# Mixer groups as steps placed by column tile, in a one-core decoder layer

## The chip, the cores and the metric

The kernel runs on one core of a Trainium2 chip. The metric is device time in microseconds (us) of one execution; of several runs the median is given. A core has five engines that run side by side and wait for one another through semaphores: PE (matrix products), DVE (elementwise), ACT (elementwise with functions), POOL (elementwise), and SP, which here issues the DMA transfers. Each engine takes its instructions strictly in the order of its own queue.

## What is computed

One decoding step of one hybrid layer, for 256 prompt tokens and 8 sampled sequences of one token, 264 columns in all: a half feed-forward step, a mixer, a second half feed-forward step, and a gated per-layer embedding. The mixer is what matters here:

```python
proj = u @ w_in
glu_a, glu_b, z, xbc, dt_raw = jnp.split(proj, [s1, s2, s3, s4], axis=-1)
v = glu_a * jax.nn.sigmoid(glu_b)
v, new_conv_buf = causal_dwconv(v, conv_buf, conv_mod_w, conv_mod_b)     # 31 taps
v = jax.nn.silu(layernorm(v, conv_mod_ln_g, conv_mod_ln_b))
xbc, new_xbc_buf = causal_dwconv(xbc, xbc_buf, ssm_conv_w, ssm_conv_b)   # 4 taps
xbc = jax.nn.silu(xbc)
xs, bm, cm = jnp.split(xbc, ...)
y, h_new = ssd(xs, dt, a, bm, cm, d_skip, h0r)
yg = y * jax.nn.silu(z)
yg = yg * lax.rsqrt(jnp.mean(yg * yg, axis=-1, keepdims=True) + EPS)     # in 8 groups
out = jnp.concatenate([v, yg * ssm_norm_g], axis=-1) @ w_out
```

`ssd` is a chunked state-space scan in 8 groups of 6 heads. For the sampled sequences it multiplies the incoming state of 64x128 per head (`h0`) with C and sums over the 128 state columns.

## The kernel before

**Matrix products.** Activations lie with channels on the 128 partitions and the 264 columns along the free axis. The weights come from memory in the order in which a list, PLAN, uses them, one unit of 16 tiles of 128x128 at a time, in two pieces of 8 tiles: SP loads a piece into `wraw`, ACT casts it into `whi` (line 152), and DVE takes the rest `wlo` = `wraw` - `whi` (line 153). Each of the three has four buffers, so the cast of a piece can begin once PE is through the piece four before it. A product of one weight tile is three matmuls (lines 248, 249, 250): `whi` with both parts of the activation and `wlo` with the first. A piece is thus 24 matmuls, and one column tile of the input projection (128 output channels over 2048 inputs) is 48. Its result is an `acc` in PSUM, of which there are five buffers.

**The input projection.** `IN_ORDER` lists its 81 column tiles: dt first, then for each of the 8 groups one tile B, one C, three x and three z. After the first x tile of the groups in `GLU_IN` stands a pair of tiles for the GLU (gb and ga), and the pairs left over come after the last group. What is done with each tile stands in the loop at lines 810 to 850. `do_conv` (line 610) reads an `acc` of B, C or x, does the 4-tap convolution on ACT and DVE and ends in a SiLU on ACT. `decays` (line 677) loads and makes the decay factors `ab` and `ea` of a group after its first x tile (DMA, ACT with Exp). After the third x tile `ssd` (line 698) does the whole group: transposes of x and B on PE (lines 708, 709), the product of B and C (722), chunk states (734), outputs (749, 756), then for the sampled sequences two transposes that give the rows of B and C (762, 763), a trip of these rows through memory to spread C over all partitions (766, 768), the product of state and C on POOL and its sum on DVE (774, 775), and the small rest. `gate` (line 790) multiplies `y` with SiLU(z) on DVE, squares three tiles on ACT (into `run` and two `tmp`), adds them on POOL into `run`, sums `run` over the channels on PE (`SumSq.total`, line 300, a matmul with a matrix of ones), takes the root through Ln and Exp on ACT and applies it. It is called for a group after the first x tile of the next one.

**GLU.** `do_glu` (line 641) takes Exp, Ln and Exp of one pair, multiplies, and puts 30 further taps of the 31-tap convolution on a list `bg`. Four entries of that list are done after each column tile, ten after each output column of the output projection. Behind the last pair's taps stands `do_ln`, the LayerNorm over the eight GLU tiles. Their first reader is the last part of the output projection (line 882).

**What sets the order.** The program text gives each instruction its priority. A scheduler that keeps a timeline of its own lays the instructions into the five queues before the run: an engine takes, of what that timeline has ready, the instruction that stands first in the text, and the weights' loads, casts and subtractions go ahead of the rest. Functions of ACT that need a table (Silu, Sigmoid, Exp, Ln) are tied to the order of the text among themselves (`after`, line 223), and a table is loaded whenever the set changes (line 236). PSUM tiles of the pool `ps` (three buffers) are handed out in the order of the text.

## Time and profile before

| | us |
|---|---|
| median of 3 runs | 2439.51 (2439.47 to 2445.9) |
| the profiled execution | 2438.53 |
| its span, first to last instruction | 2436.7 |
| input projection of the mixer, about | 842 to 1345 |
| output projection, its main part, about | 1345 to 1494 |

The span is what the views of the profile show; the execution's own time has 1.8 us around it. In a row of the stages stand the length, then for PE, PE's weight loads, DVE, ACT and POOL the busy time and the number of instructions, then the clock that PE was granted, the share of the DMA engines and GB/s. A list of waits names the engine that waited with the line of its instruction, whom it waited for, the total, how often, and the longest.

### The profile page before, as it was taken

The page shows a single profiled execution, that of the slowest core. Times are in us where ns is not written, and L with a number is a line of the kernel's source. Part 1 is how long each engine was busy: PE and PEld are TensorE (multiplying, and loading weights), DVE is VectorE, ACT ScalarE, POOL GpSimd, SP SyncE. Part 2 cuts the span into 40 slices and gives each one's busy share as a digit, 9 for nine tenths or more (in the row PEclk, how much of TensorE's full clock was granted, in tenths as well). Part 3 has the DMA queues.
Part 4 walks back from the last instruction along what each step waited for, and adds up shares of the span by engine and source line. Part 5 has one row for each costly group of instructions (what it writes and reads, how often), then busy time and mean ns, then how long its engine had stood idle before and what let it go on. Part 6 is the DMA issues. An engine that isn't in the chain of part 4 may idle for free.

```text
span 2436.7 us, 47389 instructions
## 1 busy us (share of the span) xinstructions
PE 2370.0 (97%) x19444; PEld 2343.4 (96%) x19444; DVE 1577.0 (65%) x2273; ACT 1181.7 (48%) x1765; POOL 349.8 (14%) x351
## 2 busy tenths in 40 slices
PE   8999999999999999999999999899999999999988
PEld 8999999999999899999999999899999999999988
DVE  6554455545557858979798975866555565565595
ACT  6444444433456465565655555544444443344464
POOL 2500000000015212121121011400000000000142
PEclk9999999999999999999999999999999999999999
DMA  7656555555556666676666556477766676676653
GB/s 245 215 184 184 183 183 183 183 184 183 184 170 207 210 197 191 208 222 204 205 215 197 181 178 226 139 239 235 232 208 226 227 241 217 217 234 203 192 177 132
DMA packets 165386, 489.89 MB, mean 201 GB/s; under 512 B 25472, under 2 KB 42544, under 8 KB 165168
## 3 DMA queue, kind: packets, MB, share of 16 engines
q1 hardware_dynamic: 165168, 486.86, 62.1%
q8 instruction: 152, 2.49, 0.4%
q14 instruction: 66, 0.54, 0.1%
HBM read 465.65 MB, written 22.42 MB: 200 GB/s over the span
## 4 chain that ended last, share of the span: by engine, by line
PE 81%; DVE 7%; DMA 4%; issue 3%; ACT 2%; POOL 1%; SPq 0%; POOLq 0%; ACTq 0%; DVEq 0%
PE acc L248 26%; PE acc L249 26%; PE acc L250 26%; DVE wlo L153 3%; DVE y L217 1%; DMA d_bc<-rows 1%; DMA cbc<-d_bc 1%; POOL h L214 1%; DMA s<-in_hst 1%; DMA h<-in_hst 1%; DVE h L214 1%; DVE tmp L217 1%; ACT whi L152 1%; POOL run L214 1%; DVE act L217 1%
## 5 line engine op out<-in xcount | busy, mean ns | idle before, releaser
L250 PE MATMUL acc<-act,wlo 128*128 128x264 f32 x6320 | 1796.6, 285 | 4.4 <-DVE wlo L153 4.2
L249 PE MATMUL acc<-act,whi 128*128 128x264 f32 x6320 | 1783.7, 283 | 14.7 <-DVE act L217 7.8
L248 PE MATMUL acc<-act,whi 128*128 128x264 f32 x6320 | 1767.6, 283 | 16.6 <-ACT whi L152 8.7
L153 DVE TENSOR_TENSOR wlo<-wraw,whi 128x1024 fp32r<-128x1024 f32 (+1 forms) x806 | 994.9, 1236 | 584.9 <-ACT whi L152 580.7
L152 ACT CAST whi<-wraw 128x1024 fp32r<-128x1024 f32 (+1 forms) x806 | 829.0, 1033 | 945.2 <-PE acc L249 698.4
L248 PEld LDWEIGHTS acc<-act,whi 128*128 128x128 f32 x6320 | 1191.8, 190 | 19.9 <-ACT whi L152 8.9
L249 PEld LDWEIGHTS acc<-act,whi 128*128 128x128 f32 x6320 | 1188.6, 188 | 20.4 <-DVE act L217 10.0
L250 PEld LDWEIGHTS acc<-act,wlo 128*128 128x128 f32 x6320 | 1187.3, 188 | 8.1 <-DVE wlo L153 6.1
L214 POOL TENSOR_TENSOR run<-run,tmp 128x264 f32<-128x264 f32 x135 | 129.6, 960 | 956.0 <-ACT tmp L241 952.5
L214 POOL TENSOR_TENSOR s<-s,eap 128x1024 f32<-128x1024 f32 x24 | 46.4, 1932 | 598.8 <-DMA s<-in_hst 598.8
L217 DVE SCALAR_TENSOR_TENSOR y<-v,vec,y 128x251 f32<-128x251 f32 (+23 forms) x240 | 117.3, 512 | 1.2
L217 DVE SCALAR_TENSOR_TENSOR s<-bb,xds,s 128x128 f32<-128x128 f32 x192 | 52.6, 347 | 72.8 <-POOL s L214 72.8
L214 POOL TENSOR_TENSOR h<-h,cbc 128x512 f32<-128x512 f32 x48 | 72.2, 1524 | 167.4 <-DMA cbc<-d_bc 79.6
L256 ACT CAST act<-tmp 128x264 fp32r<-128x264 f32 x120 | 48.7, 411 | 72.8 <-DVE tmp L214 58.5
L214 DVE TENSOR_TENSOR tmp<-acc,rr 128x264 f32<-128x264 f32 x104 | 44.8, 431 | 56.8 <-PE acc L250 56.8
L214 DVE TENSOR_TENSOR tmp<-tmp,acc 128x264 f32<-128x264 f32 x88 | 37.7, 428 | 40.4 <-PE acc L250 39.4
L214 DVE TENSOR_TENSOR act<-tmp,act 128x264 fp32r<-128x264 f32 x120 | 54.3, 458 | 0.0
L241 ACT ACTIVATE tmp<-tmp 128x264 f32<-128x264 f32 x112 | 47.1, 422 | 10.2 <-DVE tmp L214 9.7
L241 ACT ACTIVATE tmp<-y 128x264 f32<-128x264 f32 x67 | 28.1, 426 | 43.6 <-DVE y L214 42.5
L214 DVE TENSOR_TENSOR y<-y,acc 128x264 f32<-128x264 f32 x80 | 34.0, 425 | 23.5 <-PE acc L250 23.5
L775 DVE TENSOR_REDUCE ych<-h 128x4 f32<-128x512 f32 x48 | 32.5, 678 | 20.0 <-POOL h L214 20.0
L217 DVE SCALAR_TENSOR_TENSOR act<-h,vec,act 128x264 fp32r<-128x264 f32 x48 | 35.2, 756 | 6.1 <-ACT act L241 6.1
(155 smaller groups left out, 787.2 us busy)
## 6 DMA issues: line engine op xcount, KB each, us to landing
wraw<-in_w SPq DMA_DIRECT2D x774, 512.0 KB, 4.7
h<-in_hst SPq DMA_DIRECT2D x48, 256.0 KB, 4.0
s<-in_hst SPq DMA_DIRECT2D x24, 512.0 KB, 6.8
out_nss<-s SPq DMA_DIRECT2D x24, 512.0 KB, 2.8
wraw<-in_w SPq DMA_DIRECT2D x32, 256.0 KB, 3.9
ab<-d_cs SPq DMA_DIRECT2D x16, 384.0 KB, 4.8
cbc<-d_bc SPq DMA_DIRECT2D x8, 512.0 KB, 4.3
bb<-d_bc SPq DMA_DIRECT2D x8, 512.0 KB, 8.3
```

The source lines that it names most:

```text
L152: nc.scalar.copy(hi, raw)
L153: nc.vector.tensor_tensor(out=lo, in0=raw, in1=hi.bitcast(F32), op=ALU.subtract)
L214: return (eng or nc.vector).tensor_tensor(out=out, in0=in0, in1=in1, op=op)
L217: return nc.vector.scalar_tensor_tensor(out=out, in0=in0, scalar=scalar, in1=in1, op0=op0, op1=op1)
L241: i = nc.scalar.activation(out=out, in_=in_, func=func, bias=bias, scale=scale)
L248: nc.tensor.matmul(acc, hi, x[:, 0, :], start=first, stop=False)
L249: nc.tensor.matmul(acc, hi, x[:, 1, :], start=False, stop=False)
L250: nc.tensor.matmul(acc, lo, x[:, 0, :], start=False, stop=last)
L256: nc.scalar.copy(t[:, 0, :], x)
L775: nc.vector.tensor_reduce(out=ych[:, j, b : b + 4], in_=h0, op=ALU.add, axis=AX.X)
```

## The change

The part of `ssd` for the sampled sequences becomes functions of its own (`sample_rows`, `sample_c`, `sample_state`, `sample_out`), `gate` becomes `gate_begin` and `gate_end`, and an object for each group, made at its B tile, places these steps at numbers of column tiles: a step that is placed at `n` stands in the text behind the tile `n`. The rows of B and C are made at the C tile and no longer behind the group's other work; C is spread two tiles later; the products of state and C take three tiles, each one's sum standing one tile behind its product; `ssd` comes one tile after the third x tile; and the gate comes after the group's own last z tile, in two tiles, and no longer behind the first x tile of the next group. GLU pairs stand in the groups 1, 3 and 5 only, so five pairs and no longer four follow the last group.

```diff
-GLU_IN = (1, 2, 4, 6)
+GLU_IN = (1, 3, 5)
...
-        if i < len(GLU_IN) + 2:
+        if yp is None:
             v = apool.tile([P, T], F32, tag="v", bufs=2, name=nm("v"))
...
         tt(y[:, :, P:NP_], y[:, :, P:NP_], ea, ALU.add)
-
-        js = slice(3 * g, 3 * g + 3)
+        return y
+
+    def sample_rows(g, bf, cf):
+
         pr = ps_tile([P, 2, P])
         nc.tensor.transpose(pr[:NS, 0, :], bf[:, NP_:], ident)
         nc.tensor.transpose(pr[:NS, 1, :], cf[:, NP_:], ident)
         rows = mp.tile([P, 2, P], F32, tag="rows", bufs=1, name=nm("rows"))
         nc.scalar.copy(rows[:NS], pr[:NS])
         nc.sync.dma_start(d_bc[g].rearrange("i b n -> b i n"), rows[:NS])
+
+    def sample_c(g):
         cbc = mp.tile([P, NS, P], F32, tag="cbc", bufs=1, name=nm("cbc"))
         nc.sync.dma_start(cbc, d_bc[g, 1].partition_broadcast(P))
-        ych = mp.tile([P, 3, NS], F32, tag="ych", bufs=1, name=nm("ych"))
-        for j in range(3):
-            for b in range(0, NS, 4):
-                h0 = mp.tile([P, 4, P], F32, tag="h0", bufs=3, name=nm("h0"))
-                nc.sync.dma_start(h0, a["hst"][3 * g + j][:, b : b + 4, :])
-                tt(h0, h0, cbc[:, b : b + 4, :], ALU.mult, nc.gpsimd)
-                nc.vector.tensor_reduce(out=ych[:, j, b : b + 4], in_=h0, op=ALU.add, axis=AX.X)
+        return cbc
+
+    products = []
+
+    def sample_state(g, j, cbc, ych):
+
+        while products:
+            o, h0 = products.pop(0)
+            nc.vector.tensor_reduce(out=o, in_=h0, op=ALU.add, axis=AX.X)
+        if j == 3:
+            return
+        for b in range(0, NS, 4):
+            h0 = mp.tile([P, 4, P], F32, tag="h0", bufs=3, name=nm("h0"))
+            nc.sync.dma_start(h0, a["hst"][3 * g + j][:, b : b + 4, :])
+            tt(h0, h0, cbc[:, b : b + 4, :], ALU.mult, nc.gpsimd)
+            products.append((ych[:, j, b : b + 4], h0))
+
+    def sample_out(g, bf, cf, xt, ych, y):
...
-        return y
-
-    def gate(g, y, zs):
+
+    def gate_begin(g, y, zs):
+
         tt(y, y, zs, ALU.mult)
         sq = SumSq(3, direct=0)
         for j in range(3):
             sq.add(y[:, j, :])
+        return sq
+
+    def gate_end(g, y, sq):
         t = tmp()
         rsqrt(t, sq.total(), eps1, 1.0 / 384)
...
+    class Group:
+
+
+        def __init__(self, g):
+            self.g = g
+            self.bc = mp.tile([P, 2, T], F32, tag="bc", bufs=2, name=nm("bc"))
+            self.xt = self.zs = None
+            place = {k: n for n, k in enumerate(IN_ORDER)}
+            c = place[("C", MT_CM + g)]
+            x, z = (place[(k, m + 3 * g + 2)] for k, m in (("x", MT_X), ("z", MT_Z)))
+            at(place[("x", MT_X + 3 * g)], self.decays)
+            at(c, lambda: sample_rows(g, *self.pair()))
+            at(c + 2, self.sample_c)
+            for j in range(4):
+                at(c + 3 + j, lambda j=j: self.state(j))
+            at(x + 1, self.ssd)
+            out = max(c + 6, x + 2)
+            at(out, self.out)
+            begin = max(out, z) + 1
+            at(begin, self.begin)
+            at(begin + 1, self.end)
...
-            if j == 0:
-                finish_gate()
-                ab, ea = decays(g)
-            if j == 2:
-                y = ssd(g, bct[:, 0, :], bct[:, 1, :], xt, ab, ea)
...
+        for step in steps.pop(n, ()):
+            step()
         for _ in range(4):
             if bg:
                 bg.popleft()()
```

What the scheduler makes of it is seen in the queues. First PE at the sum of the gate of the fifth group, before the change (`run` holds the squares added up, `whi_0_13867` is the piece in use, `ps_13756` and `ps_13765` take the transposes of the next group's x):

```order
L249 MATMUL acc_13928<-act_9304,whi_8_13692 128x264
L250 MATMUL acc_13928<-act_9304,wlo_8_13693 128x264
L248 MATMUL acc_13990<-act_9190,whi_0_13867 128x264
L249 MATMUL acc_13990<-act_9190,whi_0_13867 128x264
L300 MATMUL ps_13573<-run_13564,ones 128x264
L708 MATMUL ps_13756<-ident,h_13555 128x128
L708 MATMUL ps_13765<-ident,h_13555 128x128
L250 MATMUL acc_13990<-act_9190,wlo_0_13868 128x264
```

And ACT at the squares that this sum needs, before the change (the squares are the functions of `h_13038`):

```order
L152 CAST whi_0_13867<-wraw_0_13866 128x1024
L152 CAST whi_8_13873<-wraw_8_13872 128x1024
L241 ACTIVATE run_13564<-h_13038 128x264
L241 ACTIVATE tmp_13566<-h_13038 128x264
L241 ACTIVATE tmp_13569<-h_13038 128x264
L152 CAST whi_0_13930<-wraw_0_13929 128x1024
L152 CAST whi_8_13936<-wraw_8_13935 128x1024
L241 ACTIVATE tmp_13572<-ps_13573,eps_83 128x264
```

PE has the sum two matmuls into the piece `whi_0_13867`, while ACT has the squares only behind the next piece, `whi_8_13873`. The same two places of the change, PE first (the two transposes behind the sum are now those of the rows of B and C):

```order
L250 MATMUL acc_13533<-act_9214,wlo_0_13380 128x264
L248 MATMUL acc_13533<-act_9222,whi_0_13379 128x264
L300 MATMUL ps_13351<-run_13274,ones 128x264
L764 MATMUL ps_13371<-ident,bc_13265 8x128
L765 MATMUL ps_13371<-ident,bc_13265 8x128
L249 MATMUL acc_13533<-act_9222,whi_0_13379 128x264
```

Then ACT, after the change:

```order
L152 CAST whi_0_13379<-wraw_0_13378 128x1024
L241 ACTIVATE ab_13457<-ab_13457,acs 128x128 x6
L241 ACTIVATE bc_13265<-bc_13265 128x264
L236 ACT_TABLE_LOAD
L241 ACTIVATE run_13274<-h_12993 128x264
L241 ACTIVATE tmp_13276<-h_12993 128x264
L241 ACTIVATE tmp_13279<-h_12993 128x264
L152 CAST whi_8_13385<-wraw_8_13384 128x1024
L615 COPY xo_12565<-acc_13377 128x11
```

The squares have moved ahead by a piece against the sum: both stand in `whi_0_13379`, the sum thirteen matmuls into it.

The second place is the third x tile's transposes of the fourth group. PE before the change (`h_12006` holds the group's x, `whi_0_12443` is the piece in use):

```order
L248 MATMUL acc_12573<-act_9206,whi_0_12443 128x264
L249 MATMUL acc_12573<-act_9206,whi_0_12443 128x264
L250 MATMUL acc_12573<-act_9206,wlo_0_12444 128x264
L708 MATMUL ps_12207<-ident,h_12006 128x128
L708 MATMUL ps_12216<-ident,h_12006 128x128
L248 MATMUL acc_12573<-act_9214,whi_0_12443 128x264
L708 MATMUL ps_12207<-ident,h_12006 128x128
L709 MATMUL ps_12207<-ident,bc_11863 128x128
```

And after it (`h_11885` is the x, `whi_8_12233` the piece in use):

```order
L249 MATMUL acc_12437<-act_9270,whi_8_12233 128x264
L708 MATMUL ps_12291<-ident,h_11885 128x128
L709 MATMUL ps_12291<-ident,bc_11712 128x128
L708 MATMUL ps_12300<-ident,h_11885 128x128
L709 MATMUL ps_12300<-ident,bc_11712 128x128
L250 MATMUL acc_12437<-act_9270,wlo_8_12234 128x264
```

ACT at the SiLU of that tile, after the change (the last function of `h_11885`):

```order
L152 CAST whi_0_12227<-wraw_0_12226 128x1024
L241 ACTIVATE h_11885<-h_11885 128x264
L152 CAST whi_8_12233<-wraw_8_12232 128x1024
L152 CAST whi_0_12362<-wraw_0_12361 128x1024
L152 CAST whi_8_12368<-wraw_8_12367 128x1024
L241 ACTIVATE h_11885<-h_11885 128x264
```

Before the change the second and third tile's transposes stand within one another, in the piece just behind that of the first; after it the third stands alone, and its SiLU comes two casts behind the piece that PE uses at that place.

More of the change, by code (lines that the diff above doesn't have):

```diff
@@ L809, with at, last, group @@
+    steps = {}
+    def at(n, step):
+        steps.setdefault(n, []).append(step)
+    yctx = ctx.enter_context(ExitStack())
+    yp = None
+    def last():
+        nonlocal yp
+        mctx.close()
+        yp = yctx.enter_context(tc.tile_pool(name="yp", bufs=1))
+    first = gemm_first(us, k16, 4)
+    groups = {}
+    def group(g):
+        if g not in groups:
+            groups[g] = Group(g)
+        return groups[g]
     nglu = 0
@@ L840 @@
             nglu += 1
-            if nglu == len(GLU_IN) + 1:
-                finish_gate()
-                mctx.close()
-                yctx = ctx.enter_context(ExitStack())
-                yp = yctx.enter_context(tc.tile_pool(name="yp", bufs=1))
             if nglu == CM:
                 bg.append(do_ln)
+        for step in steps.pop(n, ()):
+            step()
         for _ in range(4):
@@ L850 @@
                 bg.popleft()()
+    assert not steps
     for k in range(CM + 16, CM + 24):
```

44 lines of the change are left out of this document (29 added, 15 removed).

## The prediction

> **What bounds the kernel now.** I read the page first, then the stage that the change touches, then who is waited for in it.
>
> ```profile
> span 2436.7 us, 47389 instructions
> PE 2370.0 (97%) x19444; PEld 2343.4 (96%) x19444; DVE 1577.0 (65%) x2273; ACT 1181.7 (48%) x1765; POOL 349.8 (14%) x351
> core 0: us, PE busy (x) PEld busy (x) DVE busy (x) ACT busy (x) POOL busy (x), PEclk, DMA share, GB/s
> 842.00:1345.00 503.00, 482.62 (x3918) 466.10 (x3916) 408.43 (x699) 291.93 (x530) 96.08 (x72) 0.99 0.66 204
> 1345.00:1494.00 149.00, 148.60 (x1232) 148.15 (x1232) 117.19 (x196) 78.54 (x117) 14.34 (x14) 1.00 0.58 184
> 1400.00:1420.00 20.00, 20.00 (x169) 20.00 (x168) 19.80 (x38) 8.04 (x9) 0.75 (x1) 1.00 0.55 185
> ```
>
> PE is the bound of the whole kernel. The change lies in the input projection of the mixer, about 842 to 1345 us; there PE is busy 482.6 of 503 us and DVE 408 (81%), so 20.4 us is all that idle PE time can give back, 0.8% of the kernel. Undisturbed, PE takes 169 matmuls in 20 us, 0.118 us each, so a weight piece (eight 128x128 tiles, 24 matmuls) lasts 2.84 us and a column tile two pieces. No change of the matmuls is made, so the time moves only with what PE waits for:
>
> ```profile
> engine line waited for: us in total, times, longest us
> PE ps L300 <- POOL run L214: 12.4, 8, 3.5
> PE ps L708 <- ACT h L241: 3.6, 2, 3.2
> PE acc L250 <- DVE wlo L153: 3.1, 4, 1.2
> PE ps L734 <- ACT btm L717: 1.1, 1, 1.1
> ```
>
> More than half is one thing, eight times: the sum over channels of the gated norm (L300, a matmul with ones, one per group) stands in PE's queue before POOL has added up the squares. One by one:
>
> ```profile
> 922.09 0.49 PE L300 MATMUL ps<-run,ones 128*128 128x264 f32 x1 [3.52 <-POOL run L214]
> 985.97 0.49 PE L300 MATMUL ps<-run,ones 128*128 128x264 f32 x1 [1.30 <-POOL run L214]
> 1053.02 0.49 PE L300 MATMUL ps<-run,ones 128*128 128x264 f32 x1 [0.77 <-POOL run L214]
> 1103.24 0.49 PE L300 MATMUL ps<-run,ones 128*128 128x264 f32 x1 [1.22 <-POOL run L214]
> 1171.26 0.49 PE L300 MATMUL ps<-run,ones 128*128 128x264 f32 x1 [2.20 <-POOL run L214]
> 1227.68 0.49 PE L300 MATMUL ps<-run,ones 128*128 128x264 f32 x1 [0.71 <-POOL run L214]
> 1291.78 0.49 PE L300 MATMUL ps<-run,ones 128*128 128x264 f32 x1 [1.33 <-POOL run L214]
> 1344.50 0.49 PE L300 MATMUL ps<-run,ones 128*128 128x264 f32 x1 [1.40 <-POOL run L214]
> 1160.00:1180.00 20.00, 17.80 (x133) 17.48 (x133) 15.98 (x31) 15.39 (x25) 2.96 (x2) 0.91 0.65 210
> ```
>
> The last row shows a second cost. In the slice of the 2.20 us wait, 133 matmuls run where 169 would: 36 x 0.118 = 4.3 us are lost, 2.2 by waiting and about 2.1 because the granted clock falls (0.91 over the slice).
>
> **The change, term by term.** The sum is made against the profiled execution: 2438.5 us, the span and 1.8 us around it, 1.0 below the median of the three runs (2439.5).
>
> (a) *The gate's sums.* The same instructions run on the same engines: one DVE product, three squares on ACT, two adds on POOL, two halves of the sum on PE. What differs is their distance in the queues. I count in weight pieces, since PE consumes them at a steady pace and ACT casts them in the same order. For the eight groups of before, the sum on PE stands 0.92, 0.54, 0.96, 0.79, 0.92, 0.79, 0.42 and 0.88 pieces ahead of the piece behind which ACT has the squares; of after, 0.33, 0.42, -0.83, 0.21, -0.54, 0.25, -0.79 and 0.83 (minus: PE is past it). So ACT gains 0.59, 0.12, 1.79, 0.58, 1.46, 0.54, 1.21 and 0.05 pieces, by 2.84 us each 1.7, 0.3, 5.1, 1.6, 4.1, 1.5, 3.4 and 0.1 us. Take these from the eight waits above, none below zero: 1.8, 1.0, 0, 0, 0, 0, 0 and 1.3 stay, 4.1 us of 12.4. **-8.3 us** (bounds -12.4, all waits gone, and 0, the distance means nothing). That gate_end stands one tile behind gate_begin is not what does it: in both orders PE has the sum two to six tiles later than its place in the code.
>
> (b) *The clock behind them.* The wait of 2.20 us goes, and its loss of 2.1 us with it, of which I take **-1.8**, since the slice also holds small matmuls; the fall behind the 3.52 us wait I leave in, as 1.8 us remain of that wait. Bounds 0 and -4 (both fall away). The Trainium skill ("TensorE: Matmul & The Clock Gate", Part 1) says that the clock is halved after at least one idle window of about 3.4 us; by that the 2.20 us wait would have cost no clock and (b) would be 0. The row with 0.91 disagrees, so the row decides.
>
> (c) *DVE.* One GLU pair less among the groups takes 30 convolution taps off DVE there, and the reductions of the sample states stand a tile behind their products:
>
> ```profile
> L217 DVE SCALAR_TENSOR_TENSOR y<-v,vec,y 128x251 f32<-128x251 f32 (+23 forms) x240 | 117.3, 512 | 1.2
> L775 DVE TENSOR_REDUCE ych<-h 128x4 f32<-128x512 f32 x48 | 32.5, 678 | 20.0 <-POOL h L214 20.0
> ```
>
> That is 30 of 240 taps, 14.7 us of 117.3, and up to 20.0 us in which DVE stood behind POOL. PE gets from it only what it waited for wlo, 3.1 us in four waits: **-1.0**, bounds -3.1 and 0.
>
> (d) *New waits of PE.* The transposes of x and of the rows of B and C stand elsewhere. The third x transposes now stand 0.1 to 1.7 pieces ahead of the piece behind which their SiLU is (before: 0.1 to 1.0). What such a distance costs is shown by three rows:
>
> ```profile
> 874.94 0.64 PE L708 MATMUL ps<-ident,h 128*128 128x128 f32 x3 [0.42 <-ACT h L241]
> 863.02 0.69 PE L708 MATMUL ps<-ident,h 128*128 128x128 f32 x2 [3.19 <-ACT h L241]
> 1068.19 0.59 PE L734 MATMUL ps<-xde,btm 128*128 128x384 f32 x1 [1.06 <-ACT btm L717]
> ```
>
> The first waits 0.42 us at 1.0 pieces, the third 1.06 us at 3.0. At up to 1.7 I take 0.4 us in each of the five groups that go beyond 1.0, **+2.0**; bounds 0 and 8 (1.06 in all eight groups). The second row, the largest, is the start of the first group: SiLU waits there for the decay terms behind two trips through memory, both orders keep that, and it stays, 0.
>
> (e) *Table loads.* ACT gets 41 instead of 27, since Exp, Ln and SiLU alternate more often.
>
> ```profile
> L236 ACT ACT_TABLE_LOAD x18 | 23.1, 1283 | 0.3
> L152 ACT CAST whi<-wraw 128x1024 fp32r<-128x1024 f32 x146 | 151.4, 1047 | 99.3 <-PE acc L249 84.8 <-PE acc L250 5.2 <-DVE y L217 2.8
> ```
>
> 14 x 1.283 = 18.0 us more on ACT, which is idle 211 of the 503 us, 99 of them right before a cast (second row), where a later start costs nothing while the piece is still ahead of PE: **0**, bounds 0 and +18.0, if each load delays a cast that PE needs. The Trainium skill ("ScalarE: Activation LUTs", Table sets: the hidden batching unit) says to do all of one set before switching, and puts a switch at about 2.7 us with a drain. By it the load on ACT would be an estimated 38 us; here a load takes 1.283 us and 0.3 us idle stand before 18 of them, so the row is used.
>
> (f) *The end of the projection.* Five GLU pairs instead of four stand behind the last group, and DVE, already full there, has 14.7 us of taps more.
>
> ```profile
> 1360.00:1380.00 20.00, 20.00 (x169) 20.00 (x168) 20.00 (x38) 7.87 (x8) 0.87 (x1) 1.00 0.70 212
> 1380.00:1400.00 20.00, 20.00 (x170) 20.00 (x168) 20.00 (x40) 8.65 (x11) 0.00 (x0) 1.00 0.57 187
> 1466.23 0.78 DVE L214 TENSOR_TENSOR act<-y,act 128x264 fp32r<-128x264 f32 x2
> 1500.95 1.22 POOL L214 TENSOR_TENSOR run<-run,tmp 128x264 f32<-128x264 f32 x1 [49.99 <-ACT tmp L241]
> ```
>
> A full DVE cost PE nothing: 169 and 170 matmuls beside 20.00 us of DVE. The LayerNorm of the convolution group (last output at 1467) is moved back by two output columns, 2 x 72 x 0.118 = 17 us, to 1484. Its first reader is the last part of the output projection, whose first pair (48 matmuls, 5.7 us) ended just before the POOL add at 1501, so it starts at about 1495: 11 us of cover stay. **0**; what the LayerNorm loses beyond 11 us would be paid, bounds 0 and +5.
>
> Sum: -8.3 - 1.8 - 1.0 + 2.0 = -9.1, so 2438.5 - 9.1 = 2429.4 for a profiled execution, and 2430 on the scale of the median. That is -0.4%; a measurement of this kernel can tell about 0.3%, 7.3 us, from no change.
>
> **Rivals.** *The waits stay (no change).* The order is fixed before the run by a scheduler with its own timeline, and PE takes the sum the moment that timeline calls it ready. Then the wait is the error of that timeline for POOL, wherever the sum stands.
>
> ```profile
> L214 POOL TENSOR_TENSOR run<-run,tmp x16: 741/840/1737, 919.0 to 1343.7; 128x264 f32<-128x264 f32 x16
> ```
>
> For it: all eight waits are above zero, and two adds of 0.74 to 1.74 us stand right before each. Against it: the distance to the squares grows by 0.5 to 1.8 pieces in six groups, which the adds, the same as before, do not fill. (a) and (b) are 0 then: 2438.5 - 1.0 + 2.0 = 2439.5, on the median's scale 2440 (2436 to 2444).
>
> *The transposes take the place of the sums (slower).* The third x transposes stand in the middle of a piece while their SiLU waits behind two casts and a DVE tap. If in the five groups of (d) each waits as long as the fifth sum, 2.2 us, and drops the clock, 2.1 us, that is 5 x 4.3 = 21.5 instead of 2.0: 2438.5 - 11.1 + 21.5 = 2448.9, 2450 on the median's scale. It makes the kernel slower than before from 11.1 / 5 = 2.2 us per group on. For it:
>
> ```profile
> ACT h L241 <- DVE h L217: 19.8, 5, 5.5
> ```
>
> ACT already stands up to 5.5 us before such SiLUs until DVE has done the taps. Against it: at 1.0 and at 3.0 pieces the rows have 0.42 and 1.06 us.
>
> *Table loads reach the casts (slower).* All of (e): 2438.5 - 9.1 + 18.0 = 2447.4, 2448 on the median's scale. The skill's rule to group by set would make it so; the 99 us that ACT stands idle before casts speak against it.
>
> **How the numbers follow.** The forecast has 0.58, with its own range 2422 to 2437: 0.45 lie beyond 0.3%, 0.13 short of it. The waits stay: 0.25. The transposes: 0.10. The table loads, or a LayerNorm that comes too late: 0.07. So faster 0.45, same 0.38, slower 0.17. The range is 2421 to 2448: below it lies nearly everything going, (a) and (b) at their ends, and above it the upper halves of the two slow cases.
>
> **What would show it.** Step (a) is right if the list of PE's waits has L300 behind POOL at about 4 us with the first and the last group leading, and wrong if eight waits of over 1 us stand there. (b) is right if the granted clock has no 0.91 slice at the fifth group. (d) is wrong if L708 or the rows' transposes wait more than 5 us. (e) is wrong if ACT's casts appear as what PE waits for; (f), if PE has a gap at the start of the last part of the output projection.

## The result, and the profile after

| | before | after |
|---|---|---|
| median, us | 2441.38 (2436.42 to 2445.9, 7 runs) | 2454.23 (2449.51 to 2461.89, 7 runs) |
| profiled execution, its span | 2438.53, 2436.7 | 2454.23, 2452.5 |

The ratio of after to before is 1.0056, 95% interval 1.0042 to 1.0070: the change makes the kernel slower by 0.56%, where the prediction had 2430 us, faster by 0.4%, and a range up to 2448.

First the stages of after, in the columns of the prediction's rows (length; busy us and instructions of PE, PE's loads, DVE, ACT and POOL; granted clock, DMA share, GB/s):

```profile
span 2452.5 us, 47416 instructions
842.00:1345.00 503.00, 472.92 (x3791) 456.65 (x3790) 394.44 (x670) 304.04 (x544) 95.36 (x74) 0.97 0.63 199
1345.00:1494.00 149.00, 149.00 (x1239) 148.75 (x1238) 121.41 (x214) 72.24 (x102) 12.71 (x12) 1.00 0.57 181
1160.00:1180.00 20.00, 15.71 (x110) 15.50 (x109) 14.71 (x20) 10.90 (x20) 7.81 (x6) 0.83 0.60 191
```

In the same 503 us of the mixer PE gets through 3791 matmuls instead of 3918. These 127, at 0.118 us, are 15.0 us, and the span is 15.8 us longer: nearly the whole loss lies here, and none in the output projection behind it. Of the 15.0 us PE is idle for 9.7 (482.62 less 472.92); the other 5 go with the granted clock, 0.97 instead of 0.99. Next, what PE waits for in this stage, all rows:

```profile
PE acc L250 <- DVE wlo L153: 24.4, 10, 4.3
PE ps L764 <- ACT bc L241: 3.2, 1, 3.2
PE acc L248 <- DVE bc L217: 1.0, 1, 1.0
PE ps L300 <- POOL run L214: 0.9, 1, 0.9
PE ps L708 <- ACT h L241: 0.4, 2, 0.2
PE ps L734 <- DVE xde L214: 0.2, 1, 0.2
```

The waits at L300 have gone from 12.4 us to 0.9, as the change of distance promised. In their place one wait has grown from 3.1 us to 24.4: PE waits for `wlo`, the second part of a weight, ten times and up to 4.3 us. Of DVE's waits in the stage, the row for the reductions, of before and then of after:

```profile
DVE ych L775 <- POOL h L214: 20.0, 19, 2.9
```

```profile
DVE ych L781 <- POOL h L214: 31.1, 10, 6.3
```

19 short waits of at most 2.9 us have become ten of up to 6.3. Of ACT's waits, the row for weights that have not landed, again of before and of after:

```profile
ACT whi L152 <- DMA wraw<-in_w: 1.8, 3, 1.3
```

```profile
ACT whi L152 <- DMA wraw<-in_w: 37.3, 14, 6.2
```

From almost nothing this has grown to 37.3 us.

One group shows how these hang together. Pieces of the timeline of after, in order of time (start, duration, instruction, and in brackets how long the engine had stood idle and for whom):

```profile
1153.24 0.61 PE L300 MATMUL ps<-run,ones 128*128 128x264 f32 x2
1153.68 0.27 PE L764 MATMUL ps<-ident,bc 128*8 128x128 f32 x1
...
1154.29 0.34 ACT L767 COPY rows<-ps 8x256 f32<-8x256 f32 x1
...
1155.14 0.29 SPq L768 DMA_DIRECT2D d_bc<-rows  x1
...
1158.32 0.33 SPq L772 DMA_DIRECT2D cbc<-d_bc  x1
...
1163.96 1.30 POOL L214 TENSOR_TENSOR h<-h,cbc 128x512 f32<-128x512 f32 x1 [11.95 <-DMA cbc<-d_bc]
...
1165.29 0.69 DVE L781 TENSOR_REDUCE ych<-h 128x4 f32<-128x512 f32 x1 [6.33 <-POOL h L214]
...
1170.17 1.21 DVE L153 TENSOR_TENSOR wlo<-wraw,whi 128x1024 fp32r<-128x1024 f32 x1
...
1171.43 0.59 PE L250 MATMUL acc<-act,wlo 128*128 128x264 f32 x1 [4.29 <-DVE wlo L153]
```

PE transposes the rows of C at 1153.7; their way through memory takes 3.2 us out (1155.14 to 1158.32) and 5.6 us back (to 1163.96), and POOL's first product 1.3 more. From the transpose to the moment at which DVE can add up, it is 11.6 us, or 4.1 weight pieces (10.1 to 14.8 us over the eight groups of after, 8.9 to 12.3 us over those of before). The reduction stands too early in DVE's queue for that: DVE stands 6.33 us, the next `wlo` begins only at 1170, and PE stands 4.29. The slice around it has a granted clock of 0.83 and 110 matmuls where 169 would run. The Trainium skill ("DMA: Bandwidth & Descriptors", Anatomy of one DMA) fits, for a DMA from GpSimd's queue, 2.0 us and the bytes at 436 GB/s; for the broadcast's 128 x 4 KB that is an estimated 3.2 us by that page. Here, from SyncE's queue, 5.6 us pass until the product starts, and the measurement decides.

### The profile page after: what moved, and what is told of

The parts are those of the page before. It is cut to its first block, busy times and chain, and to the rows that moved or that the text cites. A ratio compares the mean times of both kernels' runs of the same rounds, so it can differ in the third digit from the quotient of the medians.

```text
span 2452.5 us, 47416 instructions
## 1 busy us (share of the span) xinstructions
PE 2378.7 (97%) x19444; PEld 2351.9 (96%) x19444; DVE 1573.8 (64%) x2273; ACT 1198.2 (49%) x1779; POOL 346.4 (14%) x351
## 4 chain that ended last, share of the span: by engine, by line
PE 85%; DVE 6%; DMA 3%; ACT 3%; issue 2%; POOL 1%; SPq 0%; POOLq 0%; ACTq 0%; DVEq 0%
PE acc L250 28%; PE acc L248 28%; PE acc L249 28%; DVE wlo L153 2%; DMA cbc<-d_bc 1%; ACT whi L152 1%; DVE act L214 1%; DVE tmp L217 1%; ACT ab L241 1%; DMA ab<-d_cs 1%; PE ps L749 1%; DMA d_bc<-rows 0%; DVE ych L781 0%; DVE act L217 0%; DVE h L214 0%
## 5 line engine op out<-in xcount | busy, mean ns | idle before, releaser
L249 PE MATMUL acc<-act,whi 128*128 128x264 f32 x6320 | 1787.9, 284 | 13.0 <-DVE act L217 6.5
L248 PE MATMUL acc<-act,whi 128*128 128x264 f32 x6320 | 1769.1, 283 | 16.4 <-ACT whi L152 8.2
L248 PEld LDWEIGHTS acc<-act,whi 128*128 128x128 f32 x6320 | 1195.1, 191 | 20.5 <-ACT whi L152 8.2
L249 PEld LDWEIGHTS acc<-act,whi 128*128 128x128 f32 x6320 | 1193.0, 189 | 18.8 <-DVE act L217 9.3
L217 DVE SCALAR_TENSOR_TENSOR y<-v,vec,y 128x255 f32<-128x255 f32 (+23 forms) x240 | 108.8, 482 | 0.6
L214 DVE TENSOR_TENSOR act<-tmp,act 128x264 fp32r<-128x264 f32 x120 | 64.2, 541 | 0.0
L781 DVE TENSOR_REDUCE ych<-h 128x4 f32<-128x512 f32 x48 | 32.4, 676 | 31.1 <-POOL h L214 31.1
L214 DVE TENSOR_TENSOR y<-y,acc 128x264 f32<-128x264 f32 x80 | 34.0, 425 | 23.6 <-PE acc L250 23.5
```

What stands on the lines that cost most here:

```text
L214: return (eng or nc.vector).tensor_tensor(out=out, in0=in0, in1=in1, op=op)
L217: return nc.vector.scalar_tensor_tensor(out=out, in0=in0, scalar=scalar, in1=in1, op0=op0, op1=op1)
L248: nc.tensor.matmul(acc, hi, x[:, 0, :], start=first, stop=False)
L249: nc.tensor.matmul(acc, hi, x[:, 1, :], start=False, stop=False)
L781: nc.vector.tensor_reduce(out=o, in_=h0, op=ALU.add, axis=AX.X)
```

## The theories and the experiments

The distance that the prediction counted for the gate's sums can be counted here too: from the transpose of the rows on PE (the first of the two, that of B's rows) to the first reduction on DVE, in weight pieces, by group. Before: 5.0, 4.4, 4.7, 5.0, 4.3, 4.6, 4.4, 4.8. After: 4.0, 2.3, 2.4, 3.2, 3.2, 3.5, 4.2, 3.2. The example needed 4.1. What is missing of 4.1 in after adds up to 6.9 pieces, 19.6 us; the first reductions of the eight groups stand for 29.9 us. The count gives the direction and not each single stand: the group with 2.4 pieces stands 1.5 us, the example with 3.5 stands 6.33.

**Theory 1** is that shortage: the trip of C ends too late for DVE's queue, and what stands behind the reduction (`wlo`, and by it the freeing of `wraw` and the next weight load) gets late. **Theory 2** is the 14 further table loads, and **theory 3** the order of the tiles, three GLU pairs instead of four among the groups. Two more came up on the way: **theory 5**, that whatever wait is removed comes back at another step of the group, and **theory 6**, that SP's queue is the cause (there is no number 4). All ratios are to before, on the same chip, with 95% intervals.

**e1, the reductions without their wait.**

```diff
-            nc.vector.tensor_reduce(out=o, in_=h0, op=ALU.add, axis=AX.X)
+            nc.vector.tensor_reduce(out=o, in_=vec[:, : 4 * P].rearrange("p (b n) -> p b n", b=4), op=ALU.add, axis=AX.X)
```

> The changed kernel, but the 48 reductions of the sample states read a constant tile of the same size instead of the products: the states' contribution to y is left out, VectorE does the same work and never stands behind GpSimd; 41 table loads and three GLU pairs stay as after the change. Theory 1 (VectorE, which works in order, stands at a group's first reduction until C has made its trip through memory, the split of the weight behind it gets late, and TensorE waits for wlo and loses clock): TensorE's waits for wlo fall from 25.4 us to under 4, the time to 2425 to 2435. Theory 2 (the 14 further table loads delay ScalarE's casts): the loads are all there, 2454. Theory 3 (the order of the column tiles, GLU pairs at groups 1, 3 and 5): 2454.

Measured: 2451.08 us, 1.0064 (1.0046 to 1.0083). The waits for `wlo` in the mixer are 3.6 us, as theory 1 has it, but the time is a miss for it and near the 2454 of theories 2 and 3. PE is idle for 30.4 us there, as in after (30.1): it now waits 7.9 us at L708, 6.5 at L734, 6.1 at L300 and 5.3 at L764. SP's queue shows what else became of the stand:

```profile
SPq L786 <- POOL h L214: 70.5, 41, 7.4
```

The state loads (L786) now wait in SP's queue for POOL's products, up to 7.4 us at a time, and the weight loads behind them with them: ACT's casts still wait 32.1 us for weights. The trip held up a second in-order queue, so the run does not test theory 1 alone. That SP's queue carries the loss is theory 6.

**e2, e3, gate_end one or two column tiles later.** In the change the sum over channels comes right ahead of the rows' transposes, and PSUM tiles are handed out in the order of the text; a later gate_end lets the rows go first.

```diff
-            at(begin + 1, self.end)
+            at(begin + 2, self.end)
```

> The changed kernel with gate_end one column tile later (begin + 2), one number. The sum over channels then stands behind the transposes of the rows of B and C in the code, and these come 0.6 to 4.5 weight pieces earlier in TensorE's queue; from them to the first reduction on VectorE it is 4.0, 5.7, 6.5, 7.7, 5.1, 7.0, 5.2 and 6.2 pieces (after the change 4.0, 2.3, 2.4, 3.2, 3.2, 3.5, 4.2, 3.2; before it 5.0, 4.4, 4.7, 5.0, 4.3, 4.6, 4.4, 4.8). The trip of C takes 7 to 10 us, about 3 pieces. Theory 1: VectorE's stands at the first reductions fall under 1.5 us in groups 2 to 8, waits for wlo under 4 us in all, waits for the gate's sums under 3 us, time 2425 to 2434. Theory 2: this order needs 27 table loads instead of 41, so it expects the same here and is told apart by the run with the constant tile. Theory 3: 2454.

> The changed kernel with gate_end two column tiles later (begin + 3). Rows to first reduction: 4.0, 4.7, 5.4, 5.7, 5.6, 5.7, 5.6, 6.7 pieces; 35 table loads. Theory 1: as with one tile later, 2425 to 2434, waits for wlo under 4 us. Theory 2 (loads): 8 of the 14 further loads are there, so 2444 to 2446, between the two kernels. Theory 3: 2454.

Measured: 2446.22, 1.0038 (1.0023 to 1.0053), and 2446.87, 1.0046 (1.0028 to 1.0064). In e2 the wait for `wlo` falls from 24.4 to 9.8 us, in e3 to 16.4. Both fall short of what theory 1 expected, though it has the direction. The traces show why the distance that was counted did not help: the count starts at the transpose of B's rows (L764), and the trip needs C's (L765). A later gate_end lets B's rows go earlier, but C's have to wait for the SiLU of C. The sixth group of e3, B's rows, the SiLU, C's rows and the first reduction:

```profile
1137.67 0.27 PE L764 MATMUL ps<-ident,bc 128*8 128x128 f32 x1
1142.35 0.41 ACT L241 ACTIVATE bc<-bc 128x264 f32<-128x264 f32 x1
1143.31 0.27 PE L765 MATMUL ps<-ident,bc 128*8 128x128 f32 x1
1154.98 0.69 DVE L781 TENSOR_REDUCE ych<-h 128x4 f32<-128x512 f32 x1 [5.21 <-POOL h L214]
```

Counted from C's rows, the groups of e2 have 3.7 to 5.7 pieces and those of e3 3.3 to 4.7, and from there to the end of the first product it takes 10.3 to 14.9 us, 3.6 to 5.2 pieces. DVE still stands 23.5 us at reductions in e2, and in e3 39.2, more than in after; that PE's waits for `wlo` fell all the same in e3 shows that not all of a stand reaches PE. Theory 2 wanted e3, with eight table loads more than e2, to be 10 us slower; they differ by 0.7.

**e4, the kernel before with GLU pairs 1, 3 and 5; e5, the changed kernel with 1, 2, 4, 6.**

> The kernel before with the three GLU pairs at groups 1, 3 and 5 alone; nothing of the pipeline. Distances as before the change (4.3 to 5.0 pieces), 27 table loads. Theories 1 and 2: as before, 2436 to 2444. Theory 3 (the order of the tiles costs it): 2450 to 2456.

> The changed kernel with the four GLU pairs of before (1, 2, 4, 6): the pipeline of steps alone. Rows of C to first reduction 4.0, 2.3, 2.6, 3.2, 3.4, 4.1, 4.0, 6.1 weight pieces, 41 table loads. Theory 1 (the trip of C ends too late for VectorE) alone: waits for wlo 15 to 25 us, 12 to 15 us slower than before. Theory 1 and theory 3 side by side (the pair taken out of the groups costs some 7 us by itself, as the run with the tile order alone has it in the mixer, and the reductions the rest): 5 to 9 us slower than before. Theory 3 alone: no slower than before, waits for the gate's sums and for wlo both under 5 us, 0 to 9 us faster.

Measured: e4 2450.34, 1.0053 (1.0034 to 1.0073); e5 2460.67, 1.0083 (1.0053 to 1.0113). e4 is what theory 3 asked for and a miss for theories 1 and 2; e5 is a miss for theory 3. The order alone costs something in the old kernel, and giving it back to the new one does not help it. So theory 3 is not a term that can be added or taken off. In e5 `wlo` has 21.8 us of waits, as theory 1 says. Of the loss of e4 only a part lies in the mixer:

```profile
842.00:1345.00 503.00, 480.02 (x3885) 463.17 (x3884) 398.26 (x671) 288.14 (x525) 95.81 (x71) 0.98 0.65 203
```

33 matmuls fewer than before are 3.9 us. Another part lies ahead of the mixer, where PE had a slower pace in the profiled executions of e4 and e5 (see the end): the matmul that before has at 842.0 us, e4 has at 847.9 and e5 at 847.8. By the count of matmuls, 5.9 of the 15.2 us by which e4's span is longer lie ahead of that matmul, 7.4 between it and the beginning of the output projection, and the rest behind.

**e6, e7, both mended** (four pairs and gate_end later), and **e8, the kernel before with six pairs.**

> Both mended: gate_end one column tile later and the four GLU pairs of before (1, 2, 4, 6). Rows of C to first reduction 4.0, 5.7, 7.5, 6.5, 6.7, 5.2, 6.7, 5.2 pieces, 27 table loads. Theory 1 and 3 side by side: both losses are gone and the gate's sums (12 us of waits before) stay gone, 3 to 9 us faster than before, waits for wlo under 6 us. Theory 1 alone: as the run with gate_end one tile later, 10 us slower than before. If instead the mixer gives every wait that is removed back at another place (theory 5: a group's chain through four engines is what lasts, wherever PE stands): within 4 us of before.

> As the last one with gate_end two column tiles later: rows of C to first reduction 4.0, 4.7, 5.4, 6.5, 4.7, 7.1, 7.0, 7.2 pieces, 33 table loads. Theory 1 and 3: 3 to 9 us faster than before. Theory 2 (table loads): 4 to 5 us slower than with 27 loads. Theory 5: within 4 us of before.

> The kernel before with six GLU pairs among the groups (1 to 6) instead of four; nothing of the pipeline. Theory 3 (a pair inside a group gives TensorE 11.4 us of work that waits for no group, about 5 us of waits less per pair; three pairs instead of four lost 7 us in the mixer): 5 to 12 us faster than before. Rival: the 60 further convolution taps (29 us of VectorE) among the groups make wlo late: 3 to 10 us slower, with waits for wlo over 8 us. Without a say of the pairs: within 4 us.

Measured: e6 2443.16, 1.0020 (1.0008 to 1.0033); e7 2443.35, 1.0021 (1.0006 to 1.0036); e8 2450.00, 1.0045 (1.0027 to 1.0063). Two thirds of the loss of the change are gone in e6 and e7, not all of it. For theory 5, in e6 the transposes of x (L708) wait 9.7 us where before has 3.6; against it, DVE still stood 20.1 us at reductions, so the mending was not complete. More pairs among the groups bring nothing; e8 loses at the end of the projection, where only two pairs are left behind the last group and PE waits for that group's gate. The first row of its waits from 1345 to 1530:

```profile
PE ps L300 <- POOL run L214: 4.6, 1, 4.6
```

**e9, e10, e11, the state loads from GpSimd's queue** (in the changed kernel, in e1, in e6).

```diff
-            nc.sync.dma_start(h0, a["hst"][3 * g + j][:, b : b + 4, :])
+            nc.gpsimd.dma_start(h0, a["hst"][3 * g + j][:, b : b + 4, :])
```

> The changed kernel with the 48 loads of the sample states issued from GpSimd's queue instead of SyncE's; the weights are loaded from SyncE's alone. Theory 6 (SyncE's queue works in order; the state loads stand in it for a buffer that a reduction on VectorE must free, 56 us in 35 waits, and the weights behind them land late: ScalarE's casts waited 37.3 us for weights after the change, 1.8 us before it): ScalarE's waits for weights fall under 8 us, the waits for wlo from 25.4 to 10 to 16 us (those that stand behind a group's first reduction stay, theory 1), 5 to 9 us slower than before instead of 13 to 15. Theory 1 alone: no change, 13 to 15 us slower. Theory 2 (table loads, 41 as after the change): no change.

> Both causes taken away: the reductions read a constant tile (the states' contribution to y is left out), and the state loads are issued from GpSimd's queue; 41 table loads and three GLU pairs stay. Theories 1 and 6 together are the loss: within 4 us of before or up to 8 us faster. Theory 2 or 3 (loads, or the order of the tiles) carry it: 10 to 15 us slower than before, as with the constant tile alone.

> gate_end one column tile later, four GLU pairs (1, 2, 4, 6), and the state loads issued from GpSimd's queue; 27 table loads. Without the last part it was 6 us slower than before, with 13.6 us of casts that waited for weights. Theory 6: those fall under 5 us, and it is 0 to 8 us faster than before. Theory 5 (what is removed here comes back there): within 3 us of the run without it, 3 to 9 us slower than before.

Measured: e9 2454.62, 1.0079 (1.0060 to 1.0098); e10 2443.20, 1.0033 (1.0015 to 1.0050); e11 2445.74, 1.0044 (1.0031 to 1.0058). e9 is a miss for theory 6: SP's queue is free of the state loads, and ACT's casts still wait for weights, no less than the 37.3 us of after:

```profile
ACT whi L152 <- DMA wraw<-in_w: 39.1, 13, 5.8
```

The largest row of SP's waits in e9 says for whom SP waits with these weights:

```profile
SPq L151 <- DVE wlo L153: 301.7, 115, 11.0
```

A weight can be loaded only when DVE is through with the one four before it; where DVE stands, the loads get late whatever queue they are in. The size of this row says little, since before has 191.0 us in it and only 1.8 us of ACT's waits for weights. So the state loads in SP's queue do not by themselves make ACT's 37.3 us. That DVE's stand makes them is argued here, and fits e15 below, where the state loads are in SP's queue, DVE stands 7.4 us instead of 31.1, and the same row of ACT has 6.1 us. With the wait taken from both queues (e10) the waits for `wlo` in the mixer are 0.2 us and the time drops by about half of what e1 lost. All of it does not come back: PE waits there 8.0 us at L734 and 4.3 at L749 for DVE and ACT. e11 gained nothing on e6: ACT's waits for weights fall from 13.6 to 7.4 us, and PE's at L708 rise from 9.7 to 14.7.

**e12, more table loads in the kernel before.**

```diff
+        table("silu_and_others")
```

> The kernel before with a request for SiLU's table set behind each gate, 35 table loads instead of 27; sum and rows stand where before has them within a piece. Theory 2 (each further load costs what it lasts, 1.28 us): 10 us slower than before. Theories 1 and 6: within 4 us of before.

Measured: 2466.64, 1.0133 (1.0110 to 1.0156), 30 us slower and outside what both theories said. The trace has 43 table loads, and not the 35 that were expected:

```profile
L236 ACT ACT_TABLE_LOAD x43 | 55.2, 1283 | 1.4 <-PEq L1099 0.8
```

That is 16 more than before, 20.5 us by their length, so at least some 10 of the 30 us are something else. The request also moved the order: in three groups the distance to the first reduction fell to 3.4 or 3.5 pieces, and PE waits 14.5 us at L300 and 11.5 at L734 in the mixer. The run does not separate the loads from that, and their price stays open; it shows that ACT's queue has no such room that nothing put into it counts.

**e13, e14, no trip.** C's broadcast comes from an input in the changed kernel (e13) and in the kernel before (e14).

```diff
-        nc.sync.dma_start(cbc, d_bc[g, 1].partition_broadcast(P))
+        nc.sync.dma_start(cbc, a["hst"][g][:NS, 0, :].partition_broadcast(P))
```

> The changed kernel, but C's broadcast is loaded from an input tensor of the same shape instead of the copy of its rows that went to memory: the trip is gone (the sampled outputs are computed with other numbers), the rows are still transposed, copied and stored; 41 table loads, three GLU pairs, 48 reductions that wait for their products. Theory 1 (the trip of C ends too late for VectorE's queue): waits for wlo under 4 us, ScalarE's casts wait under 10 us for weights instead of 37.3, 0 to 10 us faster than before. Theory 5 (what is removed comes back at the transposes of the group) and theory 2 (loads): waits for wlo fall as well, but other waits of TensorE in the mixer rise by 10 us or more, 6 to 15 us slower than before.

> The kernel before with the same cut: C's broadcast comes from an input tensor. In this order the sums of the gate also stand up to 1.08 weight pieces behind their squares (before: 0.42 to 0.96 ahead). Theory 1 and step (a) of the prediction: VectorE's 20.0 us behind GpSimd go, the waits for the gate's sums fall from 12.4 to under 5 us, 8 to 15 us faster than before. Theory 5: within 4 us.

Measured: e13 2450.96, 1.0050 (1.0027 to 1.0073); e14 2461.43, 1.0101 (1.0063 to 1.0139): by the time, a miss for theory 1 twice. But the traces put the loss of e13 at a place where neither kernel had one. The mixer of e13:

```profile
842.00:1345.00 503.00, 485.46 (x3946) 469.92 (x3945) 406.58 (x700) 317.50 (x567) 89.48 (x65) 0.98 0.65 201
```

A row of PE's waits from 780 to 842 us, and the first of DVE's there:

```profile
PE acc L248 <- ACT act L256: 8.0, 1, 8.0
```

```profile
DVE ych L781 <- POOL h L214: 7.3, 1, 7.3
```

In the mixer e13 runs 155 matmuls more than after and 28 more than before: without the trip the loss is gone there, and a little is gained. (This window begins earlier in e13's work, since the matmul that before has at 842.0 us comes at 857.9; counted from that matmul to the beginning of the output projection, e13 needs 3.6 us less than before, which says the same.) But the broadcast of the first group now waits for nothing, so the scheduler put that group's first reduction ahead of the end of the feed-forward step, and DVE stood 7.3 us there, with the scaling that PE waits for behind it. It is the same kind of stand at another place, and it costs more than the gain: up to that matmul e13 is 15.9 us behind before. The 8.0 us are half of it; in the same stretch PE's waits for DVE's `act` (L249) grow from 6.0 to 11.4 us. In e14 the same stand is there, 7.0 us, and the transposes of x (L708) wait 14.3 us in the mixer as well; these I did not follow up.

**e15, e16, the reductions held back**, all work kept: each stands behind a later weight piece on DVE, and the later states' loads and products three tiles later (e16 with four GLU pairs).

```diff
+HOLD = 6
...
-            nc.vector.tensor_reduce(out=o, in_=h0, op=ALU.add, axis=AX.X)
+            with tc.issue_after(ws.lo.ins):
+                nc.vector.tensor_reduce(out=o, in_=h0, op=ALU.add, axis=AX.X)
...
-                at(c + 3 + j, lambda j=j: self.state(j))
+                at(c + (3 if j == 0 else HOLD - 1 + j), lambda j=j: self.state(j))
...
-            out = max(c + 6, x + 2)
+            out = max(c + HOLD + 2, x + 2)
```

> The changed kernel, whole, with each reduction queued on VectorE behind a later weight piece, the states' second and third step three column tiles later: rows of C to first reduction 4.0, 8.7, 11.7, 14.8, 12.2, 14.5, 12.2, 13.8 weight pieces (after 2.3 to 4.2), 35 table loads, three GLU pairs. Theory 1: no stand of VectorE at a reduction over 1.5 us behind the first group, waits for wlo under 5 us, 0 to 8 us faster than before. Theory 5: 6 to 12 us slower than before, as with gate_end moved alone.

> The same with the four GLU pairs of before: 4.0, 8.7, 11.7, 11.7, 14.9, 11.8, 14.8, 12.1 pieces, 35 table loads. Theory 1: as the last, 0 to 8 us faster than before. Theory 5: 4 to 10 us slower.

Measured: e15 2435.80, 0.9989 (0.9974 to 1.0004); e16 2438.06, 0.9995 (0.9978 to 1.0011). The loss of the change is gone, by the ratios 0.67% or some 16 us, with three pairs as with four and with 35 table loads. The waits of e15 in the mixer, first PE's two largest, then DVE's at reductions (line numbers are higher by one or two):

```profile
PE ps L301 <- POOL run L215: 5.6, 4, 1.8
PE acc L251 <- DVE wlo L154: 4.7, 4, 3.0
```

```profile
DVE ych L783 <- POOL h L215: 7.4, 6, 2.9
```

DVE stands 7.4 us instead of 31.1 (once 2.9 us, where theory 1 allowed 1.5), PE waits 4.7 us for `wlo` instead of 24.4. What is not there is the forecast's gain; in this order the gate's sums of seven groups stand 0.2 to 1.0 pieces ahead of their squares again, and 5.6 us of their waits are back.

**e17, e18, both distances at once** (reductions held, and gate_end two tiles or one tile later).

> The changed kernel, whole, with the reductions held behind a later weight piece (states' second and third step two column tiles later than in the change) and gate_end two tiles later: rows of C to first reduction 4.0, 6.7, 11.3, 12.4, 11.6, 12.5, 12.9, 12.5 weight pieces; the gate's sums 0.38, -0.75, 2.0, 1.0, 2.0, 0.0, 3.0, 3.0 pieces behind their squares; 35 table loads, three pairs. Theory 1 with step (a): waits for the gate's sums under 3 us, for wlo under 6, 5 to 12 us faster than before. Theory 5 (given back at the transposes of x and at the states' matmuls): within 4 us of before.

> The same with the states three tiles later and gate_end one tile later: 4.0, 8.7, 13.5, 14.9, 13.6, 13.4, 13.6, 13.4 pieces to the first reduction; the sums 0.38, -0.21, 0, -0.25, 0, -0.25, 0, 0 pieces from their squares; 29 table loads, six fewer than the last. Theory 1 with step (a): 4 to 10 us faster than before. Theory 2 (loads at 1.28 us each): 8 us faster than the last. Theory 5: within 4 us of before.

Measured: e17 2436.01, 0.9996 (0.9983 to 1.0008); e18 2429.73 (2427.4 to 2434.54, 8 runs), 0.9971 (0.9958 to 0.9984). e17 is what theory 5 asked for and a miss for theory 1; e18 is inside theory 1's range and outside theory 5's. e18 is faster than both kernels, 7.3 us below the median of before.

With these two, the held reductions are tried in four pairs of runs, the two of a pair alike in everything else that was set: after and e15, 0.67% faster with them; e5 and e16, 0.88%; e3 and e17, 0.50%; e2 and e18, 0.67%. Table loads do not explain it: their number is 35 in both of e3 and e17, and rises from 27 to 29 from e2 to e18. What is not separated is that the later states' loads and products move together with the reductions. The mixer of e17, then of e18:

```profile
842.00:1345.00 503.00, 483.50 (x3929) 467.40 (x3928) 416.24 (x705) 305.03 (x549) 107.29 (x74) 0.99 0.66 205
```

```profile
842.00:1345.00 503.00, 485.29 (x3987) 469.82 (x3987) 421.87 (x712) 301.14 (x548) 104.57 (x74) 1.00 0.66 208
```

And what PE waits for in the mixer of e18, its rows of a microsecond and more:

```profile
PE ps L765 <- ACT bc L242: 9.5, 4, 3.6
PE ps L735 <- DVE xde L215: 2.5, 3, 0.9
PE ps L709 <- ACT h L242: 2.1, 3, 1.1
PE acc L249 <- DVE bc L218: 1.6, 1, 1.6
PE ps L301 <- POOL run L215: 1.0, 1, 1.0
```

No wait for `wlo` is left, and 1.0 us at the sums. The 69 matmuls that e18 has more than before are 8.1 us: 2.7 from less idle time (485.29 less 482.62), the other 5.4 from the pace, at a granted clock of 1.00 instead of 0.99 (counted by matmuls, from the one that before has at 842.0 us to the beginning of the output projection, the split is 2.7 and 5.8). e17 has no wait for `wlo` either and 1.2 us at the sums, but only 11 matmuls more than before. Theory 5 thus holds in part: beside the sums and `wlo`, PE was idle for 4.9 us before (20.4 - 12.4 - 3.1), for 18.3 in e17 and 16.7 in e18; nearly all that is removed at the two comes back as idle time at the transposes and the states' matmuls, and what e18 keeps in this execution is mostly clock. It is not shown that this makes the median lower: the mean granted clock over e18's eight executions is 0.9935, as over the 19 of before on the same chip, and the profiled one, with 0.995, is the slowest of the eight. So where the 7.3 us of the median come from stays open. That the two are 6 us apart goes the way of theory 2, which asked for 8, but they differ in more than their six loads.

## Why the prediction was wrong, point by point

**The step that failed is (c), DVE**, which the prediction put as: "the reductions of the sample states stand a tile behind their products", "**-1.0**, bounds -3.1 and 0". It took the 20.0 us of DVE behind POOL as something that could only shrink, since a tile lay between product and sum, and shut out a loss by its bounds. But this reduction waits for the end of a chain that starts with C's rows, and the two had come nearer in the queues: 2.3 to 4.2 pieces instead of 4.3 to 5.0, with 4.1 needed in the example. The runs show in its place 31.1 us of stand, 21 us more waits for `wlo` and 5 us of clock. e15 gives the reductions their distance, and the whole loss goes with the stand; the other three pairs of runs say the same. The prediction counted this very distance for the gate's sums and not for the reductions, though the order of both was to be seen.

**(a), the gate's sums**, -8.3: right in its direction, and a little small, 12.4 us down to 0.9 instead of 4.1. That the distance counts is seen again in e15, where it is lost and 5.6 us are back; but group by group the arithmetic did not hold. It left 1.8, 1.0 and 1.3 us in the first, second and last group, and after has 0.9, 0 and 0; the last group gained only 0.05 pieces and lost its 1.40 us all the same. PE, held up by `wlo`, may have come to these sums later; this was not tried. The rival in which those waits stay is refuted. That the gain reaches the end is another matter: in e17 and e18 these waits are gone as well, and most of the idle time stands at the transposes instead.

**(b), the clock**, -1.8: the fall behind the 2.20 us wait went, but the prediction's own sign for it, a slice at the fifth group without a fall, did not come: the 4.29 us wait for `wlo` brought it to 0.83 there. Taken over the mixer the term turned to about +5: the trace of before has the clock at half for four stretches of 3.4 us in this window, that of after for nine.

**(d), new waits of PE at transposes**, +2.0: in after 0.6 us at L708 and L734 and 3.2 at L764. The last is the start of the first group, which the prediction kept, at L708 then. The rival that priced these waits at 21.5 us did not happen in after; in e6 (L708 9.7 us), e17 and e18 a part of it did, once DVE was no longer in the way.

**(e), table loads**, 0: not settled. e12, with 16 loads more, shows a cost with other causes mixed in. That the loads carried the loss is refuted: e15 has 35 loads and is as fast as before, and the pairs e3 and e17, e2 and e18 get faster with as many loads or two more. No cast is among what PE waits for in after's mixer.

**(f), the end of the projection**, 0: right. PE is busy 149.00 of 149.00 us there, with five pairs behind the last group.

The sum failed by one term, with its sign. Two rivals made the kernel slower, but neither was this one: none looked at what stands behind a wait in DVE's queue.

## What to carry to other kernels

When a scheduler or a plan moves a step, measure for every instruction that waits on a long chain how far it now stands from the chain's start, on the engine that will wait, and compare it with the chain's length in the trace; do it for the waits that look harmless too, since in an in-order queue the price is paid by what stands behind. A wait moved off one in-order queue may only show up on the next one (DVE, then SP, then another step), so an experiment should take the chain away or give it room, not the one wait. Count from the input that the chain really starts with: here the transposes of B's rows moved and those of C's did not. Splitting work into finer steps can bring its gain only once both ends have their distance; here the sums and the reductions had to be moved together, and one of the two orders that did so (e17) was still no faster than before.

## What the runs showed of the hardware that was not expected

The pace of PE was not the same in all profiled executions, in a stage where the instructions are the same and PE never waits. The stretch from 250 to 500 us of before, then of e18:

```profile
250.00:500.00 250.00, 250.00 (x2086) 250.00 (x2085) 127.25 (x139) 103.83 (x127) 0.00 (x0) 1.00 0.57 183
```

```profile
250.00:500.00 250.00, 250.00 (x2067) 250.00 (x2066) 125.98 (x137) 102.60 (x127) 0.00 (x0) 1.00 0.56 182
```

2067 matmuls instead of 2086 are 0.9%, at a granted clock that reads 1.00 in both; e4's profile has 2066 and e5's 2067. It is PE alone: a cast of a weight piece lasts 1.05 us and a subtraction 1.23 in both. By about 780 us the difference is gone (1081 matmuls from 1400 to 1530 us in both), but e18 and e4 come to the mixer some 6 us later by it. That is over a third of what the change cost, so a single execution says little about a few microseconds, and two traces should be compared from the same matmul on, not from the same time. What sets this pace was not tried.

The clock falls in whole steps. The slices with 0.83 or 0.91 are means; in the traces the granted clock is 1.00 or 0.50, and it stays at 0.50 for 3.4 us or a small multiple of that. The stretch behind the 2.20 us wait of before, with 16 matmuls where 27 would run:

```profile
1172.70:1175.90 3.20, 3.20 (x16) 3.20 (x16) 1.30 (x3) 3.19 (x5) 0.00 (x0) 0.50 0.84 277
```

The length of a wait alone does not decide it: a wait of 2.76 us in e18, which ends at 961.9 us, brought no such stretch. What else decides it was not tried.
